# A two-queue start: loading the first image pair whole over the hardware DMA queue and casting it on chip

## The chip, the cores and the metric

The kernel runs on one core of a Trainium2 chip. The metric is device time in microseconds (us), the median of several executions. The profile describes one execution and its span is 1.7 to 1.9 us shorter than the time of the same execution. On one core a run is called slow when it is over 1.5% above the fastest run of the same kernel. All times within a run count from the start of its span.

## The reference

A 3x3 convolution with padding 1, in fp32. The weights are 90% zeros, but the kernel treats them as dense.

```python
x: (16, 64, 64, 64) fp32      weight: (128, 64, 3, 3) fp32      out: (16, 128, 64, 64) fp32
for b, co, ci, kh, kw:
    out[b, co] += weight[co, ci, kh, kw] * x_pad[b, ci, kh:kh+64, kw:kw+64]
```

## The kernel before

Two images with 64 channels each share the 128 partitions and make a "pair"; there are eight pairs. Images are used as bf16. A load that casts fp32 to bf16 on its way is issued from POOL and runs on the software DMA queue. Uncast loads and all stores are issued from SP and run on the hardware queue. The first 18 rows of pair 0 come uncast, so that matmuls can start early; the rest comes cast.

```python
w_sb = const_pool.tile([C_OUT, C_IN * KH * KW], FP32, name="w_sb")
nc.sync.dma_start(out=w_sb, in_=weight.rearrange("o i kh kw -> o (i kh kw)"))
x_head = const_pool.tile([128, HEAD, W], FP32, name="x_head")              # HEAD = 18
nc.sync.dma_start(out=x_head, in_=pair(0)[:, 0:HEAD, :])
nc.gpsimd.dma_start(out=xs[0][:, HEAD:H, :], in_=pair(0)[:, HEAD:H, :])
ident = const_pool.tile([128, 128], BF16, name="ident")
make_identity(nc, ident)                                                   # two POOL instructions
for p in range(1, NP):
    nc.gpsimd.dma_start(out=xs[p], in_=pair(p))
# ... 27 idle matmuls; the weight is cast, transposed by TensorE (9 matmuls), differences are made
cast_x(nc.vector.tensor_copy, 0, 9)          # rows 0..8 of x_head to bf16, on DVE
cast_x(nc.scalar.copy, 9, HEAD)              # rows 9..17, on ACT
# ...
for p in range(NP):
    o = [o_pool.tile([C_OUT, H, W], FP32, name="o") for _ in range(2)]     # o_pool has 7 buffers
    for blk in range(4):                     # four blocks of 16 rows
        # pair 0, block 0: "direct", 2 x 18 matmuls straight from the bf16 image
        # every other block: POOL adds even and odd rows (tile s), then 30 matmuls, ACT and DVE finish
        # (cut)
    # each image's 2 MB store is issued from SP when its four blocks are done; the last pair stores in halves
```

## Time and profile before

| | before |
|---|---|
| time, median of 3 | 127.45 us (127.39 to 127.47) |
| span of the profile | 125.7 us |
| first product matmul | 6.68 us |
| last matmul ends | 112.86 us |
| HBM traffic | 17.07 MB read, 33.55 MB written |

These are lines of the profile page of the kernel before. The long rows cut the span in 40 slices: busy share of TensorE in tenths, its granted clock in tenths, busy share of the 16 DMA engines in tenths, and what they moved. Where a load casts, that last row counts the bf16 bytes written, so 216 GB/s there means about 430 GB/s of fp32 read. The last line is a DMA issue with its size and the time from issue to landing (the moment at which the waiting engines are told that the data is there).

```profile
span 125.7 us, 2486 instructions
...
PE   6689999999999999999999999999999999990000
...
DMA  4999999999999999999999999999999999999980
GB/s 116 254 220 214 219 216 216 214 203 334 313 292 334 334 302 344 323 318 352 412 435 433 433 433 422 417 438 425 443 422 422 412 438 427 448 396 407 422 362 21
...
x_head<-in_x_dram SPq DMA_DIRECT2D x1, 576.0 KB, 5.0
```

TensorE and the DMA engines are both full almost from end to end. TensorE stops first, and the stores that are queued by then take the last four slices.

This is the chain of work that ended last, in order of time: start, duration, what.

```profile
1.18 4.97 DMA x_head<-in_x_dram
6.14 0.02 issue
6.17 0.47 DVE x L87
6.63 0.04 issue
6.68 105.00 PE ps L134 x954
```

TensorE waits for the 18 rows and their first cast, and never again for an input. In the timeline of the same kernel (start, duration, engine, line, operation, count, idle time before), the first two lines below are single pairs of weight loads in the direct block; the third sums up all the loads that follow without a gap.

```profile
11.17 0.18 PEld L134 LDWEIGHTS <-wT 64*128 64x128 bf16 x2 [0.25 <-issue]
11.59 0.18 PEld L134 LDWEIGHTS <-wT 64*128 64x128 bf16 x2 [0.25 <-issue]
...
12.45 13.64 PEld L134 LDWEIGHTS <-wT 64*128 64x128 bf16 x128 [0.25 <-issue]
```

Pairs are about 0.43 us apart until 12.45 us; afterwards 128 loads (64 pairs) fit in 13.64 us, 0.21 us a pair. TensorE runs at half speed for its first 5.8 us: its clock is still cold. (The clock record of this trace begins only at 12.60 us, at full speed; so the page's row PEclk, left out here, shows nines before that too and doesn't tell of the cold start.)

### The profile page before, as it was taken

To read this page: it belongs to the slowest core of one execution; us is meant where nothing else is said; L and a number is where in the kernel's file an instruction comes from. 1 tells how busy PE (TensorE), PEld (TensorE's weight loads), DVE (VectorE), ACT (ScalarE), POOL (GpSimd) and SP (SyncE) were. 2 spreads that over 40 slices of the span, in tenths; PEclk is the share of its full clock that TensorE was granted. 3 is DMA by queue.
4 is the path that set the end of the run, shared out by engine and by line. 5 is a ranking of instruction groups with operands and counts; after the bars stand their busy time and mean duration, and the time that the engine had idled before them with its cause. 6 is when DMAs were issued, how large, how long until landed. Compare 5 with 4: busy or idle time off the path is not lost.

```text
span 125.7 us, 2486 instructions
## 1 busy us (share of the span) xinstructions
PE 110.5 (88%) x1002; PEld 57.5 (46%) x1002; DVE 82.2 (65%) x135; ACT 38.1 (30%) x70; POOL 40.7 (32%) x45
## 2 busy tenths in 40 slices
PE   6689999999999999999999999999999999990000
PEld 6434555555555455545554555555555555540000
DVE  0452277788878787877787778777877787773000
ACT  4511533333333333332433333333333333330000
POOL 6908543333333333333333333333333330000000
PEclk9999999999999999999999999999999999997555
DMA  4999999999999999999999999999999999999980
GB/s 116 254 220 214 219 216 216 214 203 334 313 292 334 334 302 344 323 318 352 412 435 433 433 433 422 417 438 425 443 422 422 412 438 427 448 396 407 422 362 21
DMA packets 4044, 42.70 MB, mean 340 GB/s; under 512 B 448, under 2 KB 448, under 8 KB 832
## 3 DMA queue, kind: packets, MB, share of 16 engines
q1 hardware_dynamic: 2880, 34.44, 65.6%
q0 software_dynamic: 1152, 8.09, 31.3%
q8 instruction: 8, 0.13, 0.4%
q14 instruction: 4, 0.03, 0.1%
HBM read 17.07 MB, written 33.55 MB: 403 GB/s over the span
## 4 chain that ended last, share of the span: by engine, by line
PE 84%; DMA 4%; DVE 1%; issue 1%; DVEq 0%; SPq 0%
PE ps L134 84%; DMA x_head<-in_x_dram 4%; DVE o L167 1%; DVEq L213 0%; DVE x L87 0%; SPq L60 0%; DVEq L167 0%
## 5 line engine op out<-in xcount | busy, mean ns | idle before, releaser
L134 PE MATMUL ps<-x,wT 64*128 64x504 bf16 (+3 forms) x780 | 91.5, 382 | 1.2 <-DVE x L87 1.2
L167 DVE TENSOR_TENSOR o<-ps,pc 128x512 f32<-128x512 f32 x124 | 77.8, 685 | 22.1 <-PE ps L134 19.8
L134 PEld LDWEIGHTS <-wT 64*128 64x128 bf16 x966 | 53.9, 96 | 53.3 <-issue 4.5
L153 POOL TENSOR_TENSOR s<-x 128x512 bf16<-128x512 bf16 x31 | 35.6, 1151 | 60.2 <-PE ps L134 42.9
L160 ACT COPY pc<-ps 128x512 f32<-128x512 f32 x62 | 33.3, 589 | 64.0 <-issue 61.8
L134 PE MATMUL ps<-s,wT 64*128 64x512 bf16 (+1 forms) x186 | 25.6, 377 | 0.0
L148 DVE COPY o<-ps 128x512 f32<-128x512 f32 x2 | 1.4, 691 | 4.9 <-PE ps L134 4.9
L74 PE MATMUL ps<-idle_rhs 128*128 128x128 bf16 x27 | 3.1, 313 | 1.0 <-DVE idle_rhs L71 1.0
L67 POOL DMA_DIRECT2D x<-in_x_dram x7 | 3.7, 561 | 0.0
L74 PEld LDWEIGHTS <-idle_rhs 128*128 128x128 bf16 x27 | 2.8, 148 | 1.0 <-DVE idle_rhs L71 1.0
L147 ACT COPY o<-ps 128x512 f32<-128x512 f32 x2 | 1.2, 586 | 6.2 <-PE ps L134 6.2
L91 DVE CAST w_bf<-w_sb 128x192 bf16<-128x192 f32 (+1 forms) x4 | 1.1, 353 | 2.8 <-DMA w_sb<-in_weight_dram 2.8
L91 ACT ACT_TABLE_LOAD x1 | 1.3, 1283 | 0.7 <-PEq L202 0.7
L97 PE MATMUL ps<-ident,w_bf 128*128 128x128 bf16 x9 | 1.2, 309 | 0.2 <-DVE w_bf L91 0.2
L87 DVE CAST x<-x_head 128x576 bf16<-128x576 f32 x1 | 0.5, 459 | 1.3 <-DMA x_head<-in_x_dram 1.3
L91 ACT CAST w_bf<-w_sb 128x64 bf16<-128x64 f32 (+1 forms) x2 | 0.7, 420 | 1.7 <-DMA w_sb<-in_weight_dram 1.7
L97 PEld LDWEIGHTS <-w_bf 128*128 128x128 bf16 x9 | 0.8, 129 | 0.6 <-DVE w_bf L91 0.6
L101 DVE TENSOR_TENSOR wT<-ps,wT 128x384 bf16<-128x384 f32 x2 | 1.0, 546 | 0.0
L63 POOL DMA_DIRECT2D x<-in_x_dram x1 | 0.7, 696 | 0.8 <-POOLq L202 0.8
L87 ACT CAST x<-x_head 128x576 bf16<-128x576 f32 x1 | 0.7, 672 | 0.2 <-DMA x_head<-in_x_dram 0.2
L71 DVE MEMSET idle_rhs<- 128x64 uint32 x1 | 0.1, 112 | 0.8 <-PEq L202 0.8
L110 ACT CAST wT<-ps 128x384 bf16<-128x384 f32 x1 | 0.5, 478 | 0.4 <-PE ps L97 0.4
(8 smaller groups left out, 1.9 us busy)
## 6 DMA issues: line engine op xcount, KB each, us to landing
out_dram<-o SPq DMA_DIRECT2D x14, 2048.0 KB, 17.9
x<-in_x_dram POOLq DMA_DIRECT2D x7, 1024.0 KB, 29.9
out_dram<-o SPq DMA_DIRECT2D x4, 1024.0 KB, 10.2
x<-in_x_dram POOLq DMA_DIRECT2D x1, 736.0 KB, 8.6
x_head<-in_x_dram SPq DMA_DIRECT2D x1, 576.0 KB, 5.0
w_sb<-in_weight_dram SPq DMA_DIRECT2D x1, 288.0 KB, 2.9
```

Of the source, the lines that this page charges most:

```text
L67: nc.gpsimd.dma_start(out=xs[p], in_=pair(p))
L74: nc.tensor.matmul(idle_ps, idle_rhs, idle_rhs, start=True, stop=True)
L87: copy(out=xs[0][:, a:b, :], in_=x_head[:, a:b, :])
L91: copy(out=w_bf4[:, g, a:b, :], in_=w_v[:, k : k + b - a, :])
L97: nc.tensor.matmul(wps[:, j, :], src, ident, start=True, stop=True)
L101: nc.vector.tensor_tensor(out=wT[:, g], in0=wps, in1=wT[:, G1], op=SUB)
L134: nc.tensor.matmul(ps[n][:, lo:hi, c_lo:c_hi], tap(g, kw, n), src[q, a:b:step, c_lo + kw - 1 : c_hi + kw - 1], start=(i == 0), stop=(i == ...
L147: nc.scalar.copy(out=o[0][:, r0 : r0 + rows, :], in_=ps[0])
L148: nc.vector.tensor_copy(out=o[1][:, r0 : r0 + rows, :], in_=ps[1])
L153: nc.gpsimd.tensor_tensor(out=s, in0=xs[p][:, r0 : r0 + 16 : 2, :], in1=xs[p][:, r0 + 1 : r0 + 16 : 2, :], op=ADD)
L160: nc.scalar.copy(out=c, in_=shared[n])
L167: nc.vector.tensor_tensor(out=o[n][:, first : r0 + 16 : 2, :], in0=ps[n], in1=pc[n], op=ADD)
```

## The change

The intent is to take the whole of pair 0 over the hardware queue in one transfer with long packets (16 KB per partition), leaving the cast queue to the other seven pairs. The fp32 image lies in one of the seven output buffers, which is idle at the start. DVE and ACT share the cast, and 24 more idle matmuls are to keep the TensorE clock up.

```diff
-    x_head = const_pool.tile([128, HEAD, W], FP32, name="x_head")
-    nc.sync.dma_start(out=x_head, in_=pair(0)[:, 0:HEAD, :])
-    nc.gpsimd.dma_start(out=xs[0][:, HEAD:H, :], in_=pair(0)[:, HEAD:H, :])
+    x_head = o_pool.tile([128, H, W], FP32, name="o")
+    nc.sync.dma_start(out=x_head, in_=pair(0))
 ...
-    idle_ps = psum_pool.tile([128, 128], FP32, name="ps")
-    for _ in range(27):
-        nc.tensor.matmul(idle_ps, idle_rhs, idle_rhs, start=True, stop=True)
+    def keep_at_work(times):
+        idle_ps = psum_pool.tile([128, 128], FP32, name="ps")
+        for _ in range(times):
+            nc.tensor.matmul(idle_ps, idle_rhs, idle_rhs, start=True, stop=True)
+    keep_at_work(27)
 ...
-    cast_x(nc.vector.tensor_copy, 0, 9)
 ...
-    cast_x(nc.scalar.copy, 9, HEAD)
+    keep_at_work(24)
     difference(G01, ps0)
     difference(G21, ps2)
+    cast_x(nc.vector.tensor_copy, 0, 9)
+    cast_x(nc.scalar.copy, 9, 18)
+    cast_x(nc.vector.tensor_copy, 18, 34)
+    cast_x(nc.scalar.copy, 34, 50)
+    cast_x(nc.vector.tensor_copy, 50, H)
```

More of the change, by code (lines that the diff above doesn't have):

```diff
@@ L40 @@
     NP = B // 2
-    HEAD = 18
     const_pool = ctx.enter_context(tc.tile_pool(name="const", bufs=1))
```

## The prediction

> What bounds the kernel now. Two things nearly at once. The chain of waits runs from the landing of x_head (issued 1.18 us, landed 6.15) through a 0.46 us cast to an unbroken run of matmuls from 6.68 to about 112.9 (84% of the 125.7 us span). The slice view shows the DMA engines full in nearly every slice. Packet times say about 430 GB/s (cast loads counted at their fp32 size); 50.6 MB pass between 1.99 and 124.3. The last 11 us are stores still queued. But that backlog is thin: pair 6's stores are issued at 100.8, pair 5's last packet ends at 103.1. A new transfer needs about 1.2 us to its first packet (w_sb: 0.74 to 1.99), so only about 0.9 us of PE delay is hidden; beyond that the DMA engines idle before pair 6 and the end moves with the PE.
>
> What the change does. Pair 0's traffic is the same 2.1 MB; 16 KB take 611 ns uncast against 625 cast, so DMA work saves at most 0.2 us. But the first matmul now needs all 2.1 MB instead of 0.59. Alone at 429 GB/s, weight plus pair 0 would land at about 7.6. It isn't alone: pair 1's cast load is issued at about 1.8 us (before: 2.46). In before, x_head's packets slowed from 178 to about 300 ns from 3.7 us as the cast queue came in; where stores and cast loads meet later, each gets about 215 GB/s. The Trainium skill (DMA: Bandwidth & Descriptors, Queues, rings and completion order) says engines alternate between queues packet by packet; this even split agrees. With sharing from somewhere between 4.3 and 6 us, I estimate x_head lands between 9.7 and 11.8, about 10.9. After the first cast PE starts at about 11.4, 4.7 us late.
>
> The other casts cost DVE about 1.5 and ACT 1.2 us more (worked out from 9 rows: 0.46 and 0.67). They run beside the first direct block, off the path.
>
> Clock. In before the direct block runs at half speed until 12.45 (pairs of matmuls 0.43 us apart, then 0.216), a loss of about 2.8 us. The 24 extra idle matmuls (113 ns each) end near 8; then PE idles about 3 us. The clock record of before drops to 0.5 at 115.2, 2.4 us after the last matmul. The skill (TensorE: Matmul & The Clock Gate, Part 1) gives an activity window of about 3.4 us; the trace's two transitions, 102.4 us apart, are 30 such windows. So most likely PE is cold again at its start and pays 1.7 to 3.4 us; with 30% chance it is warm and gains 2.8.
>
> Sum. Cold: +4.7 start, -0.4 clock, -0.9 hidden = +3.4. Warm: about +1.0. Predicted 130.4 us, 128.3 to 132.3. Faster by over 2%: 0.02; within 2%: 0.40; slower: 0.58.
>
> What would show it. x_head issue to landing about 9.7 us instead of 5.0; first product matmul at 11.4 (10 to 12.5); pairs 0.43 us apart for some us after it (cold), or 0.216 at once (warm); last matmul 2 to 5 us later; DMA below full in a slice around 103 to 107; the tail after the last matmul 9 to 11 us instead of 12.8; no PE wait on casts after the first block.
>
> What would make it wrong. The hardware queue keeping the engines until drained (landing 7.6, PE at 8.1): then 127 to 128. The clock kept warm over the gap. A larger backlog before pair 6 than I read.

A note on its times: packet and clock times in this prediction are about 0.24 us later than the span times used in the rest of this document. In the trace of the kernel before, w_sb's first packet starts at 1.75 us and not 1.99 (1.0 us after its issue, not 1.2), the last packet ends at 124.1, and the clock falls at 115.0, 2.1 us after the last matmul. One reason was cut: it put the slowing of x_head's packets down to the cast queue. They slow from 3.5 us, while the first cast packet starts at 4.71; and in e9_split_later below, whose first cast packet starts at 7.82, the same packets slow just so (178 to 269 ns at 3.5 us). What slows them stays open.

## The result, and the profile after

| | before | after |
|---|---|---|
| time, median of 4 | 127.46 us (127.39 to 127.74) | 132.05 us (131.74 to 132.38) |
| ratio | | 1.0356 (95% interval 1.032 to 1.0393) |
| span of the profile | 125.7 us | 129.9 us |
| x_head landed | 6.14 us | 11.83 us |
| first product matmul | 6.68 us | 12.36 us |
| last matmul ends | 112.86 us | 117.89 us |

A ratio here is the mean time of one kernel's fast runs over that of the other's of the same rounds, so it is not quite the ratio of the medians. The changed kernel is 3.6% slower.

These lines of the page after answer to those of the page before:

```profile
span 129.9 us, 2535 instructions
...
PE   6921999999999999999999999999999999992000
...
PEclk9995589999999999999999999999999999999955
DMA  5999999999899999999999999999699929989990
GB/s 166 363 305 227 230 212 209 224 212 189 277 338 308 320 318 320 373 429 439 416 429 439 419 429 434 419 434 434 255 404 409 399 91 419 469 371 419 409 406 18
...
o<-in_x_dram SPq DMA_DIRECT2D x1, 2048.0 KB, 10.7
```

There is a hole in TensorE's third and fourth slice. The DMA engines, which were full throughout before, have two holes near the end (255 and 91 GB/s). The chain after:

```profile
1.18 10.65 DMA o<-in_x_dram
11.83 0.02 issue
11.85 0.47 DVE x L89
12.32 0.04 issue
12.36 104.35 PE ps L140 x954
```

The transfer takes 10.65 us instead of 4.97, and the unbroken run of matmuls starts that much later. The stretches below come from the windows view: from and to, length, busy time of PE, PEld, DVE, ACT and POOL with instruction counts, granted clock, DMA busy share, GB/s. First before:

```profile
92.00:95.00 3.00, 3.00 (x32) 1.51 (x29) 2.52 (x4) 0.83 (x3) 0.90 (x2) 1.00 1.03 437
...
104.00:107.00 3.00, 3.00 (x32) 1.50 (x29) 2.27 (x4) 1.00 (x2) 0.00 (x0) 1.00 1.01 431
```

and after:

```profile
6.73:10.14 3.41, 0.71 (x12) 0.63 (x11) 0.00 (x0) 0.00 (x0) 0.00 (x0) 1.00 1.05 327
...
92.00:95.00 3.00, 3.00 (x32) 1.53 (x30) 2.42 (x5) 1.07 (x2) 1.15 (x1) 1.00 0.56 235
...
104.00:107.00 3.00, 3.00 (x33) 1.54 (x31) 2.45 (x4) 1.07 (x2) 1.10 (x1) 1.00 0.23 98
```

In both late stretches TensorE is fully busy and the DMA engines lack work, because the stores of pairs 5 and 6 come too late: they are issued at 93.07 and 105.88 us, against 88.03 and 100.84 before. That is how a late start at the front becomes lost time at the end. The packet records, averaged over the 16 engines, show it as a sum: the engines are at work for 122.4 us in both kernels, and between 90 and 108 us they idle for 4.0 us in the changed kernel and not at all before. The span grew by 4.2. The 24 idle matmuls did warm the clock (its record is at full speed from 6.73 us), but they ended at 7.44; TensorE was busy for 0.71 us of the 3.41 from 6.73 on, and the clock record falls to 0.5 from 10.14 to 16.97. The direct block again ran cold, as these lines of the timeline after show:

```profile
5.20 2.24 PE L74 MATMUL ps<-idle_rhs 128*128 128x128 bf16 x24
...
12.36 6.24 PE L140 MATMUL ps<-x,wT 64*128 64x512 bf16 x36 [4.92 <-DVE x L89]
```

### The profile page after: what moved, and what is told of

It is laid out like the page before. It is cut to its first block, busy times and chain, and to the rows that moved or that the text cites. A ratio compares the mean times of both kernels' runs of the same rounds, so it can differ in the third digit from the quotient of the medians.

```text
span 129.9 us, 2535 instructions
## 1 busy us (share of the span) xinstructions
PE 111.8 (86%) x1026; PEld 58.4 (45%) x1026; DVE 83.5 (64%) x137; ACT 39.1 (30%) x71; POOL 40.4 (31%) x44
## 3 DMA queue, kind: packets, MB, share of 16 engines
HBM read 17.07 MB, written 33.55 MB: 390 GB/s over the span
## 4 chain that ended last, share of the span: by engine, by line
PE 80%; DMA 8%; DVE 1%; issue 1%; DVEq 0%; SPq 0%
PE ps L140 80%; DMA o<-in_x_dram 8%; DVE o L173 1%; DVEq L219 0%; DVE x L89 0%; SPq L59 0%; DVEq L173 0%
## 5 line engine op out<-in xcount | busy, mean ns | idle before, releaser
L140 PEld LDWEIGHTS <-wT 64*128 64x128 bf16 x966 | 52.7, 96 | 57.5 <-issue 7.5
L74 PE MATMUL ps<-idle_rhs 128*128 128x128 bf16 x51 | 5.3, 295 | 1.0 <-DVE idle_rhs L69 1.0
L74 PEld LDWEIGHTS <-idle_rhs 128*128 128x128 bf16 x51 | 5.0, 141 | 1.0 <-DVE idle_rhs L69 1.0
L89 DVE CAST x<-o 128x576 bf16<-128x576 f32 (+2 forms) x3 | 1.6, 589 | 5.2 <-DMA o<-in_x_dram 5.2
L65 POOL DMA_DIRECT2D x<-in_x_dram x7 | 3.9, 577 | 0.1
L89 ACT CAST x<-o 128x576 bf16<-128x576 f32 (+1 forms) x2 | 1.6, 856 | 5.9 <-DMA o<-in_x_dram 5.9
L113 DVE CAST wT<-ps 128x384 bf16<-128x384 f32 x1 | 0.6, 559 | 0.3 <-PE ps L99 0.3
## 6 DMA issues: line engine op xcount, KB each, us to landing
out_dram<-o SPq DMA_DIRECT2D x14, 2048.0 KB, 14.4
```

Of the source, the lines that this page charges most:

```text
L74: nc.tensor.matmul(idle_ps, idle_rhs, idle_rhs, start=True, stop=True)
L89: copy(out=xs[0][:, a:b, :], in_=x_head[:, a:b, :])
L140: nc.tensor.matmul(ps[n][:, lo:hi, c_lo:c_hi], tap(g, kw, n), src[q, a:b:step, c_lo + kw - 1 : c_hi + kw - 1], start=(i == 0), stop=(i == ...
```

## The experiments

The theory: the changed load costs time only by starting TensorE late. It is late because (a) the first matmul now needs 2.1 MB instead of 0.59, and (b) the hardware queue must share the DMA engines with the cast queue. TensorE's lateness then beats the small backlog of stores. The rivals: one large uncast transfer is slow by itself; casting on chip or the borrowed buffer costs; the clock, not the data, is to blame; TensorE alone bounds the kernel.

All eleven kernels gave correct results and ran in three rounds beside the kernel before, whose median was 127.37 to 127.52 us. "Last matmul" and spans come from the profiled run. Each median is of all four runs of a kernel; five runs count as slow and are left out of the ratios (131.42 us of e1, 132.91 of e6, 134.69 of e7, 130.04 and 130.12 of e10). What made them slow isn't shown; of these only the run of 130.04 us has a trace.

| run | first product matmul | last matmul ends | span | time, median | ratio to before (95%) |
|---|---|---|---|---|---|
| before | 6.68 | 112.86 | 125.7 | 127.46 | |
| after | 12.36 | 117.89 | 129.9 | 132.05 | 1.0356 (1.032 to 1.0393) |
| e1_warm | 13.47 | 116.74 | 127.8 | 129.63 | 1.0126 (1.0065 to 1.0186) |
| e2_cast_later | 10.60 | 115.56 | 127.6 | 129.30 | 1.0158 (1.010 to 1.0216) |
| e3_split | 6.78 | 118.22 | 130.1 | 132.65 | 1.0397 (1.0343 to 1.0451) |
| e4_before_held | 11.89 | 115.17 | 126.3 | 127.95 | 1.0019 (0.9985 to 1.0053) |
| e5_before_warm | 6.55 | 110.26 | 125.4 | 127.37 | 0.9975 (0.9932 to 1.0018) |
| e6_cast_last | 9.28 | 114.11 | 128.9 | 130.70 | 1.0238 (1.0171 to 1.0304) |
| e7_no_idle | 12.42 | 118.39 | 130.4 | 132.35 | 1.0335 (1.0258 to 1.0411) |
| e8_before_held_longer | 14.05 | 117.33 | 129.4 | 131.18 | 1.0274 (1.0223 to 1.0324) |
| e9_split_later | 6.97 | 114.92 | 126.8 | 128.55 | 1.0076 (1.0031 to 1.0121) |
| e10_small_cast | 10.25 | 116.16 | 128.2 | 129.39 | 1.0042 (0.996 to 1.0123) |
| e11_three_pieces | 7.12 | 112.98 | 126.0 | 127.72 | 1.001 (0.9969 to 1.0051) |

### Does an earlier or later TensorE alone move the time? (e5, e4, e8)

These three leave every load of the kernel before as it was and add idle matmuls ahead of the first product.

```diff
     nc.scalar.copy(out=wT[:, G2], in_=ps2)
+    held_ps = psum_pool.tile([128, 128], FP32, name="ps")
+    for _ in range(11):          # e4_before_held: 105, e8_before_held_longer: 153
+        nc.tensor.matmul(held_ps, idle_rhs, idle_rhs, start=True, stop=True)
```

> Kernel before with 11 more idle matmuls between the transposes and the first product, to bring the clock up earlier. Theory (before is held by the DMA engines at its end; only lateness of TensorE costs): the direct block runs partly or wholly at full speed, the last matmul comes 1 to 2.9 us earlier, the store backlog grows by the same and the time stays within 0.4 us of before. Rival (TensorE alone bounds before): the time falls by 1 us or more, by as much as the last matmul moves.

Measured: the direct block ran warm and the last matmul came 2.6 us earlier (110.26), yet the time was 127.37 against 127.41 us. The timeline of e5 shows the 36 matmuls of the direct block in 3.99 us, where before took 6.89:

```profile
6.55 3.99 PE L137 MATMUL ps<-x,wT 64*128 64x512 bf16 x36
```

So before gains nothing from an earlier TensorE: the stores hold its end.

> Kernel before, loads unchanged, with 105 idle matmuls that hold TensorE until about 12.2 us and leave it warm. Theory (the changed load acts only by the start of PE): the same time as e1_warm within 0.5 us, 129.0 to 130.0, with the DMA engines idle for 1 to 3 us before pair 6's stores. Rival (the changed load costs something besides the start): this run is over 1 us faster than e1_warm.

Measured: 127.95 us, below the expected range. TensorE was held to 11.89 us and its last matmul came 2.3 us late, but the span grew by only 0.6 us. The DMA engines did idle, for a little over 1 us in all between 102 and 105 us (the trace's packet records, summed per microsecond). So about 1.7 us of lateness was hidden here, against 0.8 in the changed kernel (+5.03 us at the last matmul, +4.2 in the span). The rival's words, over 1 us faster than e1_warm, were literally met, but TensorE started 1.58 us later in e1_warm than here and its span was 1.5 us longer. That leaves little or nothing for the load itself, but a cleaner test was needed, with TensorE as late as in the changed kernel.

> Kernel before, loads unchanged, with 153 idle matmuls that hold the first product until about 14.6 us, chosen so that a warm TensorE ends as late as in the changed kernel (last DVE addition at about 119.2). Theory (the changed load acts only by when TensorE runs): the DMA engines idle before pair 6's stores as in the changed kernel, time 130.8 to 132.3. Rival (the uncast load and on-chip casts cost more besides): under 130.

Measured: 131.18 us. The page of e8 shows the same two holes as the page after, in the same slices, although every load is that of the kernel before:

```profile
span 129.4 us, 2792 instructions
...
DMA  4999999999999999999999999999799829999990
GB/s 126 240 214 223 215 213 220 213 210 225 324 334 306 327 319 324 344 410 441 431 418 441 425 415 441 425 415 438 299 405 471 334 96 476 415 387 405 423 395 18
```

Its last matmul ends 0.56 us earlier than after's, and its span is 0.5 us shorter. Holding TensorE reproduces the loss almost whole. The two ratios differ by 0.8%, of which 0.5 us, or 0.4%, goes with the earlier last matmul; whether the other 0.4% is more than noise the times can't tell, as the intervals just overlap. The traces leave little room for it: between 90 and 108 us the DMA engines idled for 3.6 us in e8 and 4.0 in the changed kernel, and the spans grew by 3.7 and 4.2.

### Why did x_head land so late? (e6, e2, e10)

e6_cast_last and e2_cast_later make POOL wait before it issues the cast loads:

```diff
+    gate = const_pool.tile([128, 1], FP32, name="gate")
+    nc.gpsimd.tensor_copy(out=gate, in_=x_head[:, 0, 0:1])   # e2_cast_later: in_=w_sb[:, 0:1]
     for p in range(1, NP):
         nc.gpsimd.dma_start(out=xs[p], in_=pair(p))
```

> Changed kernel whose cast loads are issued only after x_head has landed (a one-element copy of x_head on POOL). Theory (x_head is late because of sharing): x_head alone lands at 7.9 to 8.6, PE starts at 8.4 to 9.1, but the DMA engines idle for 2 to 4 us before the first cast packet, which is not made up; time 129.0 to 131. Rival (a single large uncast transfer is slow by itself): x_head lands after 10.

Measured: with the engines to itself x_head landed at 8.74 us, close to the expected 7.9 to 8.6, and not at 11.83. So the transfer isn't slow by itself. Sharing cost 3.1 us: 2.4 until the last data packet (8.43 against 10.86) and 0.7 from there to the landing. But the time was 130.70: the DMA engines moved no data from 8.43 to 10.65 us, and were slow to fill again until 13.

```profile
8.00:12.00 4.00, 2.72 (x14) 1.19 (x15) 1.60 (x3) 1.62 (x2) 3.20 (x6) 0.63 0.38 39
```

That is e6's window from 8 to 12 us, with a DMA share of 0.38. TensorE's last matmul is only 1.25 us later than before's, and the span is 3.2 us longer. The DMA engines have no hole at the end here. In this kernel it isn't TensorE that costs the time, but DMA work put off at the front.

> Changed kernel whose cast loads are issued only once the weight has landed (a one-element copy on POOL waits for it, at about 3.7 us). Theory (x_head lands late because the cast loads share the DMA engines): first cast packet at 7.5 to 8.2, x_head lands at 8.0 to 8.6 instead of 11.9, PE starts at about 8.8, no idle stretch of the DMA engines, time 127.3 to 128.5. Rival (a 2.1 MB hardware-queue transfer is slow by itself): x_head still lands after 11 and the time stays at about 132.

Measured: 129.30 us, a miss. The first cast packet came at 7.5 us as expected, but x_head landed at 10.07, so TensorE started at 10.60 instead of 8.8, and the DMA engines idled for 2.1 us between 101 and 105 us where no idle stretch was expected. Two estimates were too good: in the three microseconds from 2 to 5 the hardware queue moved 300, 282 and 398 GB/s and not 429, so about 0.34 MB was still to come when the cast packets arrived; and the landing came 0.9 us after the last data packet. The direction is right: less sharing, earlier start, and a smaller loss. Against the interval of the kernel after (1.032 to 1.0393) the gain is clear.

e10_small_cast changes only the size of the first cast packets:

```diff
-    for p in range(1, NP):
+    for r in range(0, H, 16):
+        nc.gpsimd.dma_start(out=xs[1][:, r : r + 16, :], in_=pair(1)[:, r : r + 16, :])
+    for p in range(2, NP):
         nc.gpsimd.dma_start(out=xs[p], in_=pair(p))
```

> Changed kernel whose first cast load (pair 1) is issued as four loads of 16 rows, so that its packets carry 4 KB of fp32 instead of 16. Theory (the DMA engines alternate packet by packet, so the share goes by packet size): while both queues are active the hardware queue gets about four fifths instead of half, x_head lands at 9.5 to 10.4 instead of 11.9, PE starts at 10.0 to 10.9, time 129.5 to 131.0. Rival (the queues share by bytes): x_head lands at 11.5 or later and the time stays at 131.7 to 132.4.

Measured: x_head landed at 9.72 us and TensorE started at 10.25, both inside the expected ranges. The median was 129.39 us, but the four runs spread from 127.50 to 130.12 and two of them, the profiled one (130.04) too, count as slow; the two fast ones were 127.50 and 128.74, below the expected range. From the fastest to the slowest the four were granted 0.968, 0.955, 0.947 and 0.935 of the TensorE clock, so a direct block that ran more or less cold may be behind the spread; in the trace at hand (0.947) it ran cold. Its time is poorly known, then, and the ratio 1.0042 rests on the two runs with the warmer clock; but all four are faster than any run of the changed kernel (131.74 and up). The shares at the start are what this run is for. From the packet records, while both queues were active:

| run | hardware packet | cast packet (fp32 read) | hardware GB/s | cast GB/s | share of hardware | by packet size |
|---|---|---|---|---|---|---|
| after, 6 to 10 us | 16,384 B | 16,384 B | 213 | 215 | 0.50 | 0.50 |
| e3_split, 7 to 11 us | 11,776 B | 16,384 B | 180 | 247 | 0.42 | 0.42 |
| e10_small_cast, 6 to 8.5 us | 16,384 B | 4,096 B | 324 | 81 | 0.80 | 0.80 |

The Trainium skill (DMA: Bandwidth & Descriptors, Queues, rings and completion order) says that each engine takes the queues in turn, a packet at a time. The page means by a packet a bundle of, typically, 9 to 17 single moves, while a packet record of the trace is one partition's share of a transfer, so the unit need not be the same. With the trace's records as the unit, three packet ratios agree with turns to two digits: whoever has the longer packets gets the larger share. The end of the transfer agrees too: the records have sixteen four-byte writes there, as many as there are DMA engines, and then comes the landing. With the engines to itself (e6) x_head landed 0.31 us after its last data packet. In the changed kernel the writes came 0.6 us later than the data, about one cast packet (0.62 us), and x_head landed 0.96 us after its last data; in e10 it was 0.2 us, about one of its short cast packets (0.17), and 0.56.

### Is waiting for all of the pair the loss? (e3, e9, e11)

e3_split, and the extra piece of e11:

```diff
-    nc.sync.dma_start(out=x_head, in_=pair(0))
+    nc.sync.dma_start(out=x_head[:, 0:18, :], in_=pair(0)[:, 0:18, :])
+    nc.sync.dma_start(out=x_head[:, 18:H, :], in_=pair(0)[:, 18:H, :])
+    # e11_three_pieces: 18:34 and 34:H instead of 18:H
```

> Changed kernel with pair 0 in two hardware transfers, 18 rows and then 46, both uncast and cast on chip as before. Theory (the loss is that the first matmul waits for all 2.1 MB): the head lands at about 5 to 6, PE starts by about 7.5, a short wait of PE for the rows after 18 (landing at about 12) is hidden; time 127.2 to 127.9. Rival (uncast traffic, on-chip casts or the borrowed buffer cost the time): time stays above 130.

Measured: 132.65 us, a clear miss, and as slow as the changed kernel. The head did land at 5.97 us, and TensorE started at 6.78. The expected "short wait" for the other rows was the error. The chain of e3 shows it:

```profile
1.65 12.74 DMA o<-in_x_dram
14.39 0.02 issue
14.41 0.70 DVE x L90
...
15.26 1.40 POOL s L160
16.66 0.04 issue
16.70 100.34 PE ps L141 x918
```

Rows 18 and up landed at 14.39 us, later than the whole pair after: their shorter packets drew only 42% of the data rate. The cast and the row addition on POOL followed, and TensorE waited 5.9 us for its second block; meanwhile the clock went cold again. The start was repaired, and the same lateness came back one block later. By itself this run can't tell the theory from the rival that on-chip casts cost.

e9_split_later is e3 with the cast loads issued after the weight has landed, as in e2.

> Changed kernel with both remedies: pair 0 in two hardware transfers (18 rows, then 46), and cast loads issued once the weight has landed. Uncast load, borrowed buffer and on-chip casts stay. Theory (the start was lost to sharing and to waiting for all 2.1 MB): head lands at about 5, rest at about 10, PE starts at about 6.5 and waits less than 1.5 us before its second block, last matmul no later than before's 112.9, time 126.9 to 127.9. Rival (casting on chip or loading uncast costs by itself): over 129.

Measured: 128.55 us, between the theory's range and the rival's, so the time by itself decides nothing; the trace says more. Rows 18 and up landed at 11.45 us, and TensorE waited 2.8 us for its second block instead of less than 1.5. The direct block had ended at 10.96, so 0.5 us of the wait was for the landing; then came 0.7 us of cast and 1.4 us of row addition on POOL. So the on-chip cast does add to this wait, but it is the smaller part.

e11_three_pieces keeps the later cast loads of e9, brings the second block's rows as a transfer of their own and moves the last piece's casts behind the copies that take the direct block's results out of PSUM (only this last part is shown here):

```diff
-    cast_x(nc.scalar.copy, 34, 50)
-    cast_x(nc.vector.tensor_copy, 50, H)
 ...
         for blk in range(4):
+            if p == 0 and blk == 1:
+                cast_x(nc.scalar.copy, 34, 50)
+                cast_x(nc.vector.tensor_copy, 50, H)
```

> Changed kernel with pair 0 in three hardware transfers (18, 16 and 30 rows), cast loads issued once the weight has landed, and the last piece's casts placed after the direct block's evacuations on DVE and ACT. Theory (every wait of TensorE on pair 0 was the loss; with none left the stores bound the end as in before): PE starts at 6.5 to 7.2 and waits less than 0.7 us afterwards, last matmul at 110.3 to 111.5, no idle stretch of the DMA engines before pair 6, time 126.7 to 127.7, the same as before. Rival (casting on chip or the hardware queue costs by itself): over 128.3.

Measured: 127.72 us, the same as before (1.001), 0.02 us above the expected range. The DMA engines had no hole ahead of pairs 5 and 6; their row is that of the page before:

```profile
DMA  4999999999999999999999999999999999999980
```

TensorE started at 7.12 and still waited 2.4 us instead of less than 0.7, now for its third block (the last piece landed at 14.4 us); so its last matmul, expected at 110.3 to 111.5, came at 112.98, about where before has it. All the uncast traffic, the borrowed buffer and the on-chip casts are still in this kernel. So they cost nothing that shows, once TensorE isn't late at its end. Nor do they gain anything: no version here beats the kernel before, which agrees with e5.

### What did the clock cost? (e1, e7)

```diff
-    keep_at_work(24)
+    keep_at_work(95)             # e7_no_idle: the line is taken out
```

> Changed kernel with 95 instead of 24 idle matmuls in the gap, so that TensorE is busy until just before x_head lands. Theory (late start, cold clock and a thin store backlog add up): first product matmul still at about 12.4 us, but pairs 0.216 us apart at once; last matmul about 2.4 us earlier than in the changed kernel; time 129.3 to 130.0. Rival (the clock state at the start doesn't reach the end, because stores bound the end): time stays at 131.7 to 132.4.

Measured: 129.63 us (fast runs 128.34 to 129.71). In the profiled run x_head landed later than after, at 12.93, yet the last matmul came 1.15 us earlier: the direct block took 3.99 us instead of 6.24.

```profile
5.17 5.53 PE L74 MATMUL ps<-idle_rhs 128*128 128x128 bf16 x95
...
13.47 3.99 PE L140 MATMUL ps<-x,wT 64*128 64x512 bf16 x36 [2.77 <-DVE x L89]
```

So the clock is a real term of about 2.3 us in the changed kernel, but only because TensorE is late there; in e5 the same gain bought nothing. The two kernels' intervals don't overlap.

> Changed kernel without the 24 idle matmuls. Theory (in the changed kernel they end 5 us before the first product and the clock is lost again): x_head lands at 11.4 to 13, the direct block starts at half speed as in the changed kernel, time 131.3 to 132.7, no clear difference. Rival (they save part of the warm-up): over 133.

Measured: 132.35 us, no clear difference from the changed kernel (1.0258 to 1.0411 against 1.032 to 1.0393), with the first product at 12.42 us and cold. The 24 idle matmuls end too early to help.

## Why the prediction was right

The time, 132.05 us, lies in the stated range of 128.3 to 132.3, near its upper end; slower by over 2% was held most likely, and it came out at 3.6%.

- What bounds before: right. e5 shows that an earlier TensorE gains nothing, and e4 and e8 show that a later one costs after a small allowance.
- DMA work unchanged: right. Both pages list 17.07 MB read and 33.55 MB written, and the DMA engines are at work for 122.4 us in both kernels. No version with the uncast load was faster than before, and e11 ties with it.
- Sharing by packets in turn: right, shown by the three shares and by e6.
- The start, +4.7 us: right in kind, too small. It was +5.68 (12.36 less 6.68). x_head's last data packet ended at 10.86, at the central estimate of 10.9 for the landing. What was not foreseen is the landing itself, which came 0.96 us later, at 11.83. The four-byte completion writes came 0.6 us after the last data of the engines, which is about the length of one cast packet; with the engines to itself (e6) the whole step from the last data to the landing took 0.31 us, as in before (0.30).
- The clock, -0.4 us if cold: right; from first product to last matmul the changed kernel took 0.65 us less than before (105.53 against 106.18). The 30% chance of a warm start didn't come about; the predicted 130.4 lies 0.45 us below the cold case (127.45 + 3.4).
- Hidden, -0.9 us: right for the changed kernel (5.03 us at the last matmul became 4.2 us in the span). Other runs hid up to 1.8 us (e1, e4), for a reason that stays open.
- Sum: +5.68 - 0.65 - 0.83 = +4.2 us in the span, against +3.4 in the cold case. The mis-sized term is the start (5.68 against 4.7), and in it the step from the last data to the landing.
- Two details were wrong. The tail after the last matmul was predicted at 9 to 11 us, which contradicts the prediction's own 0.9 us (12.8 less 0.9 is 11.9); it was 12.0. And the DMA engines ran dry twice, ahead of pair 5 too, where only pair 6 had been named.
- The on-chip casts off the path: right for the changed kernel, where TensorE waits for casts only once. In e3, e9 and e11, where pieces arrive late, a cast lies in the wait.

## What to carry to other kernels

When a first transfer gates everything, count what its consumer needs first, and then which other queue will be running packets beside it: the share follows the packet sizes, so a rival queue with packets as long as one's own halves the rate (0.50 here), and shorter pieces of one's own get a smaller share (0.42 here). Before valuing a later or earlier start, measure the backlog at the far end: here a TensorE 2.6 us earlier was worth nothing, while one 5 us later cost 4.2. Repairing the first wait alone can simply move it to the next block, so follow the chain on to the next consumer.

## What the Trainium skill lacked or had wrong

- DMA: Bandwidth & Descriptors (Specifications) gives about 1 us to the first byte of a software-queue transfer. Behind a busy hardware queue, the first cast packet came 4.2 us after POOL began its first cast issue (1.43 to 5.63 us, changed kernel); with idle engines it came after 1.4 us (9.21 to 10.65, e6).
- The same page (Anatomy of one DMA, written for the software queue) calls the semaphore write nearly free. For the hardware queue's x_head, on engines shared with 16 KB packets, it came about 0.6 us after the data, and the landing 0.96 us after the last data (changed kernel); in e1, where one last write came at 12.5 us, the landing slipped to 12.93 us, 1.9 us after the last data. With the engines to itself (e6) the landing came 0.31 us after the last data, and the write at once.
- The same page names packet-by-packet turns, but not what follows from them when the packets of two queues differ in length: shares of 0.50, 0.42 and 0.80 at packet ratios of 1:1, 0.72:1 and 4:1. Its preferred packet of at most 4,096 B (SWDGE vs HWDGE vs iDMA) isn't what the records show here: cast packets of 16,384 B read and 8,192 B written, if a record is at most one packet.
- TensorE: Matmul & The Clock Gate (Part 1) speaks of an idle window of about 3.4 us before the clock falls. It fell here at the end of windows of that length that were partly busy: 0.71 us of 3.41 in the changed kernel, 1.27 at the end of before and 1.40 in e10 (5.38 to 8.79 us); it held after one with 1.47 (e7, 116.92 to 120.33 us). No other window at full clock in these traces lies between the last two.
